# The passage from retention to the last MLP of a two-layer diffusion trunk: token chains in another order, two tokens scaled together, two weight units split earlier

## The chip, the cores and the metric

The kernel runs on one core of one Trainium2 chip, in float32. A core has a matrix engine (TensorE, PE in the profile, its weight loads PEld), three engines for element-wise work (VectorE or DVE, ScalarE or ACT, GpSimd or POOL) and SyncE (SP), which here only issues DMAs. Each engine works through its own queue in order. The metric is the device time of one execution in microseconds (us).

## The reference

Two layers work on 512 latent tokens of width 1024 and on 256 context tokens. Layer 0 mixes with neighbourhood attention and spatial gating, layer 1 with a bidirectional retention of 8 heads. After each mixer stands the same kind of MLP. What lies around the change, in full precision:

```
x = x + g1 * rmsnorm(y_lat, norm_g[i, 1])            # y_lat: output of the mixer
h = modulate(rmsnorm(x, norm_g[i, 2]), sh2, sc2)     # x * (1 + scale) + shift
x = x + g2 * rmsnorm(conv_ffn(h, ...), norm_g[i, 3])

def conv_ffn(h, w_in, conv_w, conv_b, w_out):        # w_in: 1024 x 5632, w_out: 2816 x 1024
    a = dwconv3(h @ w_in, conv_w, conv_b)            # three taps along the tokens
    gate, up = jnp.split(a, 2, axis=-1)
    return (silu(gate) * up) @ w_out
```

The retention ends in `(silu(g) * normed o) @ w_out`, with `w_out` of 2048 x 1024. The normalisations go over a token's whole width, so `h` of a token can be made only when its whole row of `y_lat` is there.

## The kernel before

**Precision and units.** Every float32 operand is split into a high and a low part, and every product is three matmuls, hi x hi, hi x lo and lo x hi (`mm3`, L152). `split` (L110) makes the two: ACT writes the high part, DVE the low one. A weight unit is 128 x 1024 numbers: loaded on SP into one of three `raw` buffers (`raw_unit`, L114), then split into a slot. In retention the slots are `w0` to `w5`, handed out in turn (`slot`, L133). `rv`, `sd`, `kd`, `gt` are retention's own tiles (values, scores, keys, gated output).

**The order on the engines.** The kernel is written in program order, and a planner with a model of the engines orders each queue: of what it takes to be ready it takes the earliest in the program. An instruction issued while its engine's `hold` flag is on is pinned behind the instruction traced before it on that engine:

```
def issue(*args, **kw):
    i = f(*args, **kw)
    if self.hold:
        self.tc.keep_in_program_order(i)
    return i
```

That is class `Ordered` (L61); `self.V`, `self.S` and `self.T` are DVE, ACT and PE through it, and `hold(on)` (L367) sets all three flags. GpSimd and SP have none.

**The passage.** `retention` (L1115) ends in `out_last` (L635). It has two feature groups, A (head 6) and B (head 7, whose weights `rwo7` it gets by a call), and four tiles of 128 tokens. For tokens 0 and 1 it makes A first and holds it in PSUM (`wrA`), then adds B; for tokens 2 and 3 it makes A and B together (`wrC`). After each half row it calls `final(t, y, n)` of the `finisher` (L650), under hold. Its steps for a token: `square_half` (ACT, sum of squares of a half), `gated_rows` (DVE, product with the gate, then GpSimd's reciprocal root `yd0r` to `yd3r`), `second` = `residual` (DVE adds to `xd`, ACT sums squares, the row is stored by a DMA on ACT's queue, GpSimd makes `xd0r` to `xd3r`), `third` = `normed` (half on DVE, half on ACT). `third` also puts building of the MLP's input on a list: pieces of `MLP_PIECES` (L37), as (half, tokens, first column, last of its half). A piece (`build_piece`, L483) is a generator: PE transposes (`ht`), scalings with shift into `sa` or `sb`, at the end of a half the splits into `hb` or `b`, and two adds. `fill(n)` (L409) runs n steps of the list, `need` (L404) all of a half; `FILLS` (L42) says how many steps follow each half row. With `split=True`, `out_last` flushes token 1 (its `second` and `third`) right after its last half row. `flush` at the end takes `between`, which loads and splits `wp101` and `wp011`; `early` does that for `wp001` before group B.

**The MLP.** `ffn` (L1439) replaces the product `h @ w_in` by seven products of half-size blocks, with block sums of the input (`block_sums`, L540, tiles `blk` and `hs`) and of the weights (units `wa`, `wb`, `wc`, in the first MLP `wd`). `plain` (L1595) does the first two column blocks without that: four groups `pf` on the first half of the features (units `wp001`, `wp101`, `wp011` and the unit of `f111r`), then four groups `pf..b` on the second half (tiles `b` and `hb`), and calls `block_sums` on the way. Then comes a loop over 20 blocks: X, Y, X, Z, X, Y, X of 12 matmuls each (`px`, `py`, `pz`), with pieces of the output product (`wf`) between them, and jobs of adaLN (`ag`, `ac`, `at`) now and then. The last groups go through `out_last` again (`wf0A` and so on).

Of the kernel before, what the change touches and what calls it, by code (L numbers as in the profile page):

```python
# [9 lines left out]
F32R = mybir.dt.float32r  # L10
# [3 lines left out]
ALU = mybir.AluOpType  # L14
AX = mybir.AxisListType

P = 128
# [7 lines left out]
NF = 22  # L25
# [8 lines left out]
EARLY = 2  # L34
# [1 line left out]
Q1, Q3 = 16, 48  # L36
MLP_PIECES = (  # L37
    ((0, (4, 5), 0, False), (0, (0,), 256, True), (1, (1,), 0, False), (1, (2,), 128, False), (1, (3,), 256, True)),
    ((0, (0,), 0, False), (0, (1,), 128, True), (1, (2,), 0, False), (1, (3,), 128, True)),
)  # L40

FILLS = {  # L42
    None: ((1, 1),) * 6,
    0: ((0, 0), (0, 0), (0, 0), (3, 2), (3, 2), (0, 3)),
    1: ((0, 0), (0, 0), (0, 3), (0, 5)),
}


# [30 lines left out]
class Trunk:  # L79
# [403 lines left out]
    def build_piece(self, l, half, toks, c0, last, xn, ab):  # L483
        S, V = self.S, self.V
        w = P * len(toks)
        s = 1 if toks[0] > 3 else 0
        q = 512 // w
        pts = {}

        def turn(kk):  # L490
            pt = pts[kk] = self.ps(f"ht{l}{toks[0]}{kk}", "BC"[kk % 2], (P, q, w))
            for i in range(q):
                k = q * kk + i
                for j, t in enumerate(toks):
                    self.T.transpose(pt[:, i, j * P : (j + 1) * P], xn[t][:, k * P : (k + 1) * P], self.ident)

        def scaled(kk):
            for i in range(q):
                k = q * kk + i
                A, B = ab[:, s, 0, k : k + 1], ab[:, s, 1, k : k + 1]  # L500
                h = self.staged(l, half, k, 1)[:, 0, c0 : c0 + w]
                if kk % 2 == 0:
                    S.activation(h, pts[kk][:, i, :], AF.Identity, scale=A, bias=B)
                else:
                    V.tensor_scalar(out=h, in0=pts[kk][:, i, :], scalar1=A, scalar2=B, op0=ALU.mult, op1=ALU.add)

        for kk in range(KD // q):
            if kk:
                scaled(kk - 1)
            turn(kk)  # L510
            yield
        scaled(KD // q - 1)
        yield
        if not last:
            return
        if half:
            n = self.bn
            self.b12 = [
                [self.xp.tile([P, 2, n], F32R, name=f"b12{l}{x}{m}", tag=f"g{x}", bufs=4 if l else 3) for m in range(2)]
                for x in range(2)  # L520
            ]
        for m in range(4):
            src = self.staged(l, half, 2 * m, 2)
            if half and m < 2:
                self.split(self.b12[0][m], self.b12[1][m], src)
            else:
                b = self.blk[(11, 21)[m // 2] if not half else 22]
                ks = slice(2 * (m % 2), 2 * (m % 2) + 2)
                self.split(b[:, 0, ks, :], b[:, 1, ks, :], src)
            if m % 2:  # L530
                yield
        if not half:
            for m in (0, 2):
                b11, b21 = (self.staged(l, 0, k + m, 2) for k in (0, 4))
                if l:
                    V.tensor_tensor(out=b21, in0=b21, in1=b11, op=ALU.add)
                else:
                    self.G.dma_start(b21, b11, accum_op=ALU.add)

    def block_sums(self, l):  # L540

        V, n = self.V, self.bn
        put = lambda b, m, src: self.split(b[:, 0, 2 * m : 2 * m + 2, :], b[:, 1, 2 * m : 2 * m + 2, :], src)
        st = [[self.staged(l, h, k + 2 * m, 2) for h in (0, 1) for k in (0, 4)] for m in range(2)]

        def add(out, x):
            if l:
                V.tensor_tensor(out=out, in0=out, in1=x, op=ALU.add)
            else:
                self.G.dma_start(out, x, accum_op=ALU.add)  # L550

        for m, (b11, b21, b12, b22) in enumerate(st):
            if l:
                t1 = self.t2k(f"t1{l}{m}", shape=(P, 2, n))
            else:
                t1 = self.bp.tile([P, 2, n], F32, name=f"t1{l}{m}", tag=f"y{1 + m}", bufs=1)
            V.tensor_tensor(out=t1, in0=b11, in1=b12, op=ALU.add)
            V.tensor_tensor(out=b22, in0=b22, in1=b12, op=ALU.add)
            put(self.blk["t", 1], m, t1)
            put(self.blk["t", 3], m, b22)  # L560
            if l:
                V.tensor_tensor(out=b12, in0=b22, in1=b21, op=ALU.add)
            else:
                add(b21, b22)
                self.G.dma_start(b12, b21)
            add(b22, b11)
            if l:
                yield
        if not l:
            yield  # L570
        hb = self.bp.tile([P, 6144 + Q1], F32R, name=f"hs{l}", tag="h1", bufs=1)
        for i, x in enumerate((2, 4)):
            self.blk["t", x] = hb[:, 8 * n * i : 8 * n * (i + 1)].rearrange("p (x k c) -> p x k c", x=2, k=4)
        self.rest = hb[:, 16 * n + Q1 : 16 * n + Q1 + 2048] if l else None
        for k, x in ((4, 2), (0, 4)):
            for m in range(2):
                put(self.blk["t", x], m, self.staged(l, 1, k + 2 * m, 2))
        yield
# [53 lines left out]
        for p in self.out_pieces(*args, **kw):  # L632
            p()

    def out_last(self, A, B, y, toks, early, final, name, split=False, between=None):  # L635

        e, o = toks[:early], toks[early:]
        held = {}
        self.out_group(*A, y, e, False, None, f"{name}A", "CB", held=held)
        if callable(B):  # L640
            B = B()
        if self.early:
            self.early()
        self.out_group(*B, y, e, False, final, f"{name}B", held=held)
        if split:
            final.flush()
        self.out_group(A[0] + B[0], A[1] + B[1], y, o, False, final, f"{name}C", "A")
        final.flush(between)

    def finisher(self, gates, src, ab, name, xts, last=False, mlp=None):  # L650
# [38 lines left out]
        def fin(t, y, n):  # L689
            if n == 0:  # L690
                begin(t, y)
                self.square_half(rows[-1], 0)
                if mlp is not None:
                    self.fill(steps[len(rows) - 1][0])
                if len(rows) > 1 and not state["flushed"]:
                    second(rows[-2])
                if mlp is None:
                    self.fill(steps[len(rows) - 1][0])
            else:
                self.square_half(rows[-1], 1)  # L700
                self.gated_rows(rows[-1])
                self.fill(steps[len(rows) - 1][1])
                if len(rows) > 1 and not state["flushed"]:
                    third(rows[-2])
                state["flushed"] = False

        state = {"flushed": False}

        def flush(between=None):

            self.hold(True)
            if between:
                between()
            second(rows[-1])
            if mlp is None:
                self.fill(2)
            third(rows[-1])
            self.hold(False)
            state["flushed"] = True

        fin.flush = flush
        return fin
# [392 lines left out]
    def retention(self, y, final):  # L1115
        S, V, T, G, a = self.S, self.V, self.T, self.G, self.a
        KS = float(np.float32(P) ** np.float32(-0.5))
        with ExitStack() as ctx:
# [226 lines left out]
            def w_out(h):  # L1345
                return [self.unit(a["ret_out"][(2 * h + f) * P : (2 * h + f + 1) * P], f"rwo{h}{f}") for f in range(2)]
# [3 lines left out]
            for h in range(8):  # L1350
# [69 lines left out]
                if h < 7:  # L1420
                    wk = qk(h + 1, 8, "k")
                else:
                    self.turn += 3
                    o6 = f, w_out(6)
                    self.bg_all()
                within(h, 0)
                across(h, 0)
                across(h, 1)
# [3 lines left out]
                across(h, 2)  # L1432
                across(h, 3)
                norm(h)
            self.out_last(o6, lambda: (gated(7), w_out(7)), y, toks, EARLY, final, "r", True, self.between)
            self.between = None


    def ffn(self, l, y, final, gates=None):  # L1439
# [13 lines left out]
        with ExitStack() as ctx:  # L1453
# [141 lines left out]
            def plain(js, steps):  # L1595
# [27 lines left out]
                for x, (j, i) in enumerate(order):  # L1623
# [4 lines left out]
                    ps[j, i] = [self.ps(f"pf{l}{i}{j}", "A", (P, n))]  # L1628
                    product(ps[j, i][0], d[j, i][0], hb(11), "open")
                    product(ps[j, i][0], d[j, i][1], hb(21), "close")  # L1630
                    self.hold(x < 2)
                    if x < 2:
                        self.fill(2)
                    self.hold(False)
                sums = self.block_sums(l)
                for j in js:
                    for i in range(2):
# [165 lines left out]
    def build(self):  # L1803
# [15 lines left out]

        def hook(*units):  # L1820
            def go():
                self.early = None
                for u in units:
                    ahead(*u)

            return go
# [28 lines left out]
        y = {}  # L1855
        xts = lambda: (self.xp, ("kd0", "kd1"), 1)

        self.early = hook(("wp001", ("ffn_in", 44), 2))
        self.between = hook(("wp101", ("ffn_in", 44 + NF), 0), ("wp011", ("ffn_in", 45), 1))
        self.retention(y, self.finisher(g3, xd, self.ab[1, 1], "d", xts, mlp=1))  # L1860
        g4 = self.gate_tiles(1, 2, 1)
        self.jobs = [self.ada_half(1, h, 1, g4, side=True) for h in (10, 11)]
# [112 lines left out]
```

## Time and profile before

| | us |
|---|---|
| median of 3 runs | 1856.04 (1852.79 to 1858.48) |
| the profiled execution | 1852.3 |
| its span, first to last instruction | 1850.5 |
| PE busy / PEld busy | 1781.8 / 1582.7 |
| DVE / ACT / POOL busy | 1391.1 / 1029.3 / 330.0 |
| first MLP's loop | from 435 to 897 |
| last `wrC` of retention starts to first product of the last MLP's loop | 1468.7 to 1510.2 |
| last MLP's loop | from 1510 to about 1819 |

In a timeline row stand the start and the length in us, the engine, the kernel's line (L71 is the helper `issue`, through which all PE, DVE and ACT instructions go), the operation, output<-inputs, the shape, the count of instructions merged, and in brackets the idle time of the engine before it with what ended it. In a row of windows stand the window and its length, then busy time with the number of instructions for PE, PEld, DVE, ACT and POOL, the granted PE clock as a share of full speed, the busy share of the DMA engines and GB/s. In a row of DMA issues stand output<-input, the queue, the count, the size and the median time from issue to landing.

### The profile page before, as it was taken

The page shows a single profiled execution, that of the slowest core. Times are in us where ns is not written, and L with a number is a line of the kernel's source. Part 1 is how long each engine was busy: PE and PEld are TensorE (multiplying, and loading weights), DVE is VectorE, ACT ScalarE, POOL GpSimd, SP SyncE. Part 2 cuts the span into 40 slices and gives each one's busy share as a digit, 9 for nine tenths or more (in the row PEclk, how much of TensorE's full clock was granted, in tenths as well). Part 3 has the DMA queues.
Part 4 walks back from the last instruction along what each step waited for, and adds up shares of the span by engine and source line. Part 5 has one row for each costly group of instructions (what it writes and reads, how often), then busy time and mean ns, then how long its engine had stood idle before and what let it go on. Part 6 is the DMA issues. An engine that isn't in the chain of part 4 may idle for free. (4 is left out here: it accounts for less than half of the span.)

```text
span 1850.5 us, 28777 instructions
## 1 busy us (share of the span) xinstructions
PE 1781.8 (96%) x10928; PEld 1582.7 (86%) x10928; DVE 1391.1 (75%) x2347; ACT 1029.3 (56%) x1866; POOL 330.0 (18%) x462
## 2 busy tenths in 40 slices
PE   7999899999999999999999999999999889999997
PEld 4888777679998899998888988988999789989996
DVE  4877675789878788787866676676656699988886
ACT  6533455677555565564664534344434467766763
POOL 1102122131122322222112011011101100222221
PEclk9999999999999999999999999999999989999999
DMA  7344321155577777786722422331321225877762
GB/s 297 112 141 143 117 82 36 55 171 148 178 156 168 174 175 161 156 173 151 265 97 92 143 99 80 125 113 58 105 69 60 101 82 157 215 197 201 171 161 97
DMA packets 84399, 253.45 MB, mean 137 GB/s; under 512 B 11026, under 2 KB 11538, under 8 KB 84260
## 3 DMA queue, kind: packets, MB, share of 16 engines
q1 hardware_dynamic: 55044, 191.27, 30.9%
q0 software_dynamic: 26912, 51.95, 16.4%
q10 hardware_dynamic: 2304, 8.39, 1.1%
q8 instruction: 86, 1.41, 0.3%
q14 instruction: 53, 0.43, 0.1%
HBM read 191.80 MB, written 39.85 MB: 125 GB/s over the span
## 5 line engine op out<-in xcount | busy, mean ns | idle before, releaser
L71 DVE SCALAR_TENSOR_TENSOR acc<-ar,cs,acc 128x512 f32<-128x512 f32 x256 | 185.7, 751 | 33.7 <-DMA ar<-in_adaw 24.7
L71 DVE SCALAR_TENSOR_TENSOR cv<-pre,cw,cv 128x769 f32<-128x769 f32 (+1 forms) x176 | 153.6, 884 | 4.9 <-ACT cv L71 4.2
L71 PE MATMUL rn<-rwv,h0c 128*128 128x256 f32 x768 | 136.3, 281 | 3.0 <-ACT h0c L71 3.0
L71 PEld LDWEIGHTS rn<-rwv,h0c 128*128 128x128 f32 x768 | 118.2, 191 | 3.7 <-ACT h0c L71 3.4
L71 PE MATMUL wf<-fo,g 128*128 128x512 f32 x432 | 112.6, 394 | 0.5 <-DVE fo L71 0.5
L71 PE MATMUL rn<-rwv,h1c 128*128 128x256 f32 x384 | 108.1, 282 | 0.4 <-DVE h1c L71 0.2
L1688 POOL DMA_DIRECT2D yf<-yp x64 | 55.1, 861 | 257.0 <-ACT yp L71 233.8
L71 ACT ACTIVATE cv<-pre,cw 128x770 f32<-128x770 f32 (+1 forms) x88 | 81.3, 925 | 24.0 <-DVE pre L71 23.4
L71 PE MATMUL rn<-rwg,h0c 128*128 128x256 f32 x512 | 90.0, 280 | 0.0
L71 PEld LDWEIGHTS wf<-fo,g 128*128 128x128 f32 x432 | 75.9, 188 | 13.8 <-DVE fo L71 1.4
L71 PE MATMUL px<-hs,wc 128*128 128x384 f32 (+1 forms) x480 | 79.3, 314 | 5.4 <-ACT pre L71 3.2
L71 PEld LDWEIGHTS px<-hs,wc 128*128 128x128 f32 x480 | 74.3, 191 | 10.8 <-ACT pre L71 5.4
L71 ACT ACTIVATE pre<-px 128x256 f32<-128x256 f32 (+2 forms) x160 | 54.3, 367 | 47.7 <-PE px L71 47.6
L71 ACT COPY yp<-wf 128x512 f32<-128x512 f32 x118 | 67.8, 576 | 19.0 <-PE wf L71 16.5
L71 PEld LDWEIGHTS rn<-rwg,h0c 128*128 128x128 f32 x512 | 78.1, 189 | 0.0
L71 PE MATMUL pz<-hb,wa 128*128 128x384 f32 (+1 forms) x480 | 77.3, 308 | 0.0
L71 PE MATMUL px<-hb,wa 128*128 128x384 f32 (+1 forms) x480 | 77.1, 308 | 0.0
L71 PE MATMUL py<-blk,wb 128*128 128x384 f32 (+1 forms) x480 | 76.9, 308 | 0.0
L71 PE MATMUL px<-blk,wb 128*128 128x384 f32 (+1 forms) x480 | 76.7, 309 | 0.0
L71 PEld LDWEIGHTS px<-hb,wa 128*128 128x128 f32 x480 | 73.2, 188 | 3.2
L71 PEld LDWEIGHTS px<-blk,wb 128*128 128x128 f32 x480 | 73.4, 189 | 3.0 <-ACT pre L71 0.2
L71 PEld LDWEIGHTS rn<-rwv,h1c 128*128 128x128 f32 x384 | 72.9, 190 | 1.5 <-DVE h1c L71 1.3
(1272 smaller groups left out, 5112.6 us busy)
## 6 DMA issues: line engine op xcount, KB each, us to landing
ar<-in_adaw SPq DMA_DIRECT2D x96, 512.0 KB, 3.9
yf<-yp POOLq DMA_DIRECT2D x64, 256.0 KB, 4.2
yd<-yp POOLq DMA_DIRECT2D x54, 256.0 KB, 5.0
yd<-ypg POOLq DMA_DIRECT2D x54, 256.0 KB, 4.9
fin<-xd SPq DMA_DIRECT2D x8, 512.0 KB
xn<-in_x SPq DMA_DIRECT2D x6, 512.0 KB, 4.6
xb<-in_x SPq DMA_DIRECT2D x6, 512.0 KB
xd<-xb ACTq DMA_DIRECT2D x6, 512.0 KB, 2.8
```

The source lines that it names most:

```text
L71: i = f(*args, **kw)
L1688: G.dma_start((yd[t] if first else y[t])[:, o], v, accum_op=ALU.add)
```

## The change

- Token chains: the flush of token 1 amid `out_last` goes (`split`, `flushed`). Each token's `second` and `third` now run while the next token's half rows come in, and in this passage the filling follows `third`. The five steps that complete the first half follow token 3's first half row and no longer its second.
- The pieces of tokens 2 and 3 become one of 256 columns.
- `wp101` and `wp011` are loaded and split in head 7, ahead of its `within` (`self.ahead()`), no longer in the last flush. For that `rwo7` leaves the slots `w0` and `w1`: its first unit goes into head 7's `rv` tiles, its second, in two halves, into the `sd` tiles.
- In layer 1 the adds `b21 += b11` (two) and `b22 += b11` (two) go from DVE to accumulating DMAs on GpSimd's queue, as layer 0 has them.
- In `plain`, filling between the `pf` groups remains for the first MLP alone; the lines that set `hold` move with it.

```
-    ((0, (0,), 0, False), (0, (1,), 128, True), (1, (2,), 0, False), (1, (3,), 128, True)),
+    ((0, (0,), 0, False), (0, (1,), 128, True), (1, (2, 3), 0, True)),
 ...
-    1: ((0, 0), (0, 0), (0, 3), (0, 5)),
+    1: ((0, 0), (0, 0), (0, 3), (5, 0)),
 ...
             for m in (0, 2):
                 b11, b21 = (self.staged(l, 0, k + m, 2) for k in (0, 4))
-                if l:
-                    V.tensor_tensor(out=b21, in0=b21, in1=b11, op=ALU.add)
-                else:
-                    self.G.dma_start(b21, b11, accum_op=ALU.add)
+                self.G.dma_start(b21, b11, accum_op=ALU.add)
 ...
-            add(b22, b11)
+            self.G.dma_start(b22, b11, accum_op=ALU.add)
 ...
         if self.early:
             self.early()
+            self.early = None
         self.out_group(*B, y, e, False, final, f"{name}B", held=held)
-        if split:
-            final.flush()
         self.out_group(A[0] + B[0], A[1] + B[1], y, o, False, final, f"{name}C", "A")
         final.flush(between)
 ...
-                if len(rows) > 1 and not state["flushed"]:
+                if len(rows) > 1:
                     second(rows[-2])
 ...
                 self.gated_rows(rows[-1])
-                self.fill(steps[len(rows) - 1][1])
-                if len(rows) > 1 and not state["flushed"]:
+                if mlp != 1:
+                    self.fill(steps[len(rows) - 1][1])
+                if len(rows) > 1:
                     third(rows[-2])
-                state["flushed"] = False
+                if mlp == 1:
+                    self.fill(steps[len(rows) - 1][1])
 ...
                     o6 = f, w_out(6)
                     self.bg_all()
+                    self.ahead()
                 within(h, 0)
 ...
-            self.out_last(o6, lambda: (gated(7), w_out(7)), y, toks, EARLY, final, "r", True, self.between)
+            def last_out():
+                u = [rp.tile([P, 1536], F32R, name=f"wo7{x}", tag=f"rv{x}", bufs=1)[:, :1024] for x in range(2)]
+                halves = [[rp.tile([P, 512], F32R, name=f"wo7s{x}{n}", tag=f"sd{x}", bufs=2) for n in range(2)] for x in range(2)]
+                rows = [self.raw_unit(a["ret_out"][(14 + f) * P : (15 + f) * P], f"rwo7{f}") for f in range(2)]
+                self.split(u[0], u[1], rows[0])
+                for n in range(2):
+                    self.split(halves[0][n], halves[1][n], rows[1][:, 512 * n : 512 * n + 512])
+                return [u, [Halves(x) for x in halves]]
+
+            self.out_last(o6, lambda: (gated(7), last_out()), y, toks, EARLY, final, "r", self.between)
 ...
                     product(ps[j, i][0], d[j, i][0], hb(11), "open")
                     product(ps[j, i][0], d[j, i][1], hb(21), "close")
-                    self.hold(x < 2)
-                    if x < 2:
+                    if first and x < 2:
+                        self.hold(True)
                         self.fill(2)
-                    self.hold(False)
+                        self.hold(False)
 ...
-        self.between = hook(("wp101", ("ffn_in", 44 + NF), 0), ("wp011", ("ffn_in", 45), 1))
+        self.ahead = hook(("wp101", ("ffn_in", 44 + NF), 0), ("wp011", ("ffn_in", 45), 1))
```

More of the change, by code (lines that the diff above doesn't have):

```diff
@@ L544, in block_sums @@
         st = [[self.staged(l, h, k + 2 * m, 2) for h in (0, 1) for k in (0, 4)] for m in range(2)]
[L546 to L550, printed above, removed]
         for m, (b11, b21, b12, b22) in enumerate(st):
@@ L563, in block_sums @@
             else:
-                add(b21, b22)
+                self.G.dma_start(b21, b22, accum_op=ALU.add)
                 self.G.dma_start(b12, b21)
-            add(b22, b11)
+            self.G.dma_start(b22, b11, accum_op=ALU.add)
             if l:
@@ L633, in out_group, with out_last @@
             p()
-    def out_last(self, A, B, y, toks, early, final, name, split=False, between=None):
+    def out_last(self, A, B, y, toks, early, final, name, between=None):
         e, o = toks[:early], toks[early:]
@@ L701, in fin @@
                 self.gated_rows(rows[-1])
-                self.fill(steps[len(rows) - 1][1])
-                if len(rows) > 1 and not state["flushed"]:
+                if mlp != 1:
+                    self.fill(steps[len(rows) - 1][1])
+                if len(rows) > 1:
                     third(rows[-2])
-                state["flushed"] = False
-        state = {"flushed": False}
+                if mlp == 1:
+                    self.fill(steps[len(rows) - 1][1])
         def flush(between=None):
@@ L718, in flush @@
             self.hold(False)
-            state["flushed"] = True
         fin.flush = flush
@@ L1821, in go @@
             def go():
-                self.early = None
                 for u in units:
```

## The prediction

> **What bounds the kernel now.** I read the page first, then the table of windows by stage, then the timeline of the passage engine by engine. The page's lines of engine totals and of DMA issues that I use, with one of a list of DMA issues around 400 us:
>
> ```profile
> span 1850.5 us, 28777 instructions
> PE 1781.8 (96%) x10928; PEld 1582.7 (86%) x10928; DVE 1391.1 (75%) x2347; ACT 1029.3 (56%) x1866; POOL 330.0 (18%) x462
> yf<-yp POOLq DMA_DIRECT2D x64, 256.0 KB, 4.2
> sa<-sa POOLq DMA_DIRECT2D x2, 384.0 KB, 7.0
> ```
>
> The windows (length, then busy us of each engine with its count, granted clock, DMA share, GB/s):
>
> ```profile
> 600.00:800.00 200.00, 198.23 (x1027) 182.41 (x1026) 162.11 (x234) 115.89 (x198) 52.05 (x66) 0.99 0.77 168
> 640.63:644.04 3.41, 3.41 (x11) 2.92 (x10) 3.41 (x7) 2.64 (x4) 1.21 (x2) 0.50 0.88 208
> 1475.00:1482.00 7.00, 1.00 (x5) 0.47 (x3) 6.52 (x15) 5.49 (x16) 1.96 (x5) 0.88 0.26 106
> 1480.31:1487.14 6.83, 5.83 (x25) 5.54 (x26) 6.83 (x12) 4.87 (x8) 0.43 (x1) 0.50 0.07 8
> 1517.86:1524.68 6.82, 5.84 (x24) 5.36 (x25) 6.82 (x11) 3.45 (x6) 0.00 (x0) 0.50 0.26 77
> 1560.00:1835.00 275.00, 272.62 (x1877) 251.11 (x1876) 237.52 (x370) 184.56 (x329) 59.10 (x71) 1.00 0.71 179
> ```
>
> TensorE (PE) bounds nearly everything: 99% in the first MLP's loop (600 to 800) and in the last one's (1560 to 1835), so a microsecond that PE loses there is a microsecond of the end. The passage is the exception: one busy us of seven from 1475, then 6.8 us at clock 0.50, and once more from 1517.86. PE's rows there, with the idle time before each:
>
> ```profile
> 1468.73 5.71 PE L71 MATMUL wrC<-rwo,gt 128*128 128x512 f32 x24
> 1474.27 1.04 PE L71 MATMUL ht<-ident,yr 128*128 128x128 f32 x8
> 1481.16 6.00 PE L71 MATMUL pf<-hb,wp 128*128 128x256 f32 x24 [5.85 <-ACT hb L71]
> 1496.12 2.90 PE L71 MATMUL pf<-hb,wp 128*128 128x256 f32 x22 [0.74 <-DVE wp L71]
> 1498.85 0.28 PE L71 MATMUL pf100b<-b,wp 128*128 128x256 f32 x1
> ...
> 1513.33 1.41 PE L71 MATMUL pz<-hb,wa 128*128 128x256 f32 x11
> 1517.84 0.58 PE L71 MATMUL px<-hs,wc 128*128 128x256 f32 x1 [2.18 <-ACT wc L71]
> 1520.10 1.65 PE L71 MATMUL px<-hs,wc 128*128 128x256 f32 x6
> ```
>
> There are two holes: 5.85 us before the first `pf` (the tokens' scaled and split halves are late), and the wait for `hs` and `wc` at 1517.84, after which the same product really runs from 1520.10.
>
> **The change part by part.**
>
> *Token chains.* Rows of VectorE (DVE), ScalarE (ACT) and its queue (ACTq):
>
> ```profile
> 1471.12 0.49 DVE L71 TENSOR_SCALAR yr<-xd,xd1r 128x512 f32<-128x512 f32 x1 [1.89 <-POOL xd1r L329]
> 1471.52 1.28 DVE L71 TENSOR_TENSOR yr<-wrC,yr 128x512 f32<-128x512 f32 x2
> 1473.06 1.31 DVE L71 TENSOR_TENSOR yr<-yr,G 128x512 f32<-128x512 f32 x2 [0.25 <-ACT jyd L71]
> ...
> 1488.28 0.33 ACTq L71 DMA_DIRECT2D xd<-xd  x1
> 1493.75 1.06 ACT L71 ACTIVATE wp<-f111r 128x1024 fp32r<-128x1024 f32 x1 [2.95 <-DMA xd<-xd]
> 1494.84 1.23 DVE L71 TENSOR_TENSOR wp<-f111r,wp 128x1024 fp32r<-128x1024 f32 x1 [3.64 <-ACT wp L71]
> ...
> 1514.36 0.69 DVE L71 TENSOR_TENSOR sb<-sb,sa 128x512 f32<-128x512 f32 x1
> 1519.35 0.69 DVE L71 TENSOR_TENSOR hs<-sb,hs 128x512 fp32r<-128x512 f32 x1
> ```
>
> Today token 1 is finished in one go, so token 2's two adds and two gate products (1.28 + 1.31) stand behind a 1.89 us wait for GpSimd's `xd1r`, with their results long in PSUM. Laced, they run inside that wait, and what follows comes about 2.6 us sooner. The five steps of tokens 0/1 now precede token 2's residual: `pf` starts near 1477, not 1481.16, which leaves a hole of 1 to 2 us before it, as the last `wrC` ends a little later than now (the eight `ht` of row 1474.27 move in between). Out of DVE's way there go also the two moved splits (1.2 each, the form of row 1494.84) and an add into `sa` (0.69, the form of row 1514.36). Token 3's residual lands about 3.5 us sooner. Bounds: 0.7 (one add alone) and 5.7 (2.6 + 2.4 + 0.7); I take 3.5, from walking the pinned DVE order with these durations, since token 2's residual now stands behind the splits. Its store, issued at 1488.28, keeps `wp<-f111r` waiting until 1493.75, 5.5 us. This stays, as do the pinned scales behind it.
>
> *Last two tokens together.* Eight scalings of 256 columns take the place of sixteen of 128; saved DVE and ACT time, about 1 us each, lies behind the same wait. PE must now do all 16 transposes between the third and fourth `pf` group, when it waits anyway. No change on the path.
>
> *Two weight units and `ret_out` 7.* `wp101` and `wp011` go to the place where `rwo70` and `rwo71` are split today, early in head 7, in exchange for the same work: cost nothing. But `rwo7` must wait for head 7's `rv` and `sd` tiles, that is for its last `ro` product, and as its raw tiles hold two of three buffers, `wp001` (split at 1428.61 today) follows it. Three units' low halves, 3 x 1.23 = 3.7 us of DVE, come into the stretch of these rows:
>
> ```profile
> 1428.61 1.23 DVE L71 TENSOR_TENSOR wp<-wp001r,wp 128x1024 fp32r<-128x1024 f32 x1 [2.53 <-ACT wp L71]
> 1454.00 0.73 DVE L71 TENSOR_SCALAR on<-of,rmv,rrr 128x256 f32<-128x256 f32 x2 [0.86 <-POOL rrr L1309]
> 1456.55 1.41 DVE L71 SCALAR_TENSOR_TENSOR gt<-rt,gng,gt 128x512 fp32r<-128x512 f32 x2 [1.14 <-ACT gt L71]
> 1458.59 0.69 DVE L71 TENSOR_TENSOR yr<-wrA,yr 128x512 f32<-128x512 f32 x1 [0.63 <-PE wrA L71]
> ```
>
> The gaps shown hold 2.6 us of the 3.7, so token 0's add is late by 1.1 at most, by 0.4 if the chain's own order shields it; I take 0.8. The first `b` product then starts 2.7 us sooner.
>
> *Adds on GpSimd's DMA queue.* Four DVE adds of 0.69 leave. The last, at 1514.36, is also the last reader of the memory that `hs` takes. A DMA of this size lands in 4.2 us (`yf<-yp`), up to 7.0 (`sa<-sa`, larger). DVE has 4.3 us of other work between the rows at 1514.36 and 1519.35, so 4.2 is covered and 7.0 would cost 2.7. With two of the adds gone from the queue after `b` the product of 1520.10 starts near 1516.8 (2.7 + 1.4 - 0.8 for `hs` work bunched behind the DMA).
>
> *The order of PE.* This is no part of the change's name. In `plain` the closing `self.hold(False)` moves inside `if first and x < 2`; after the last of the four products `T.hold` stays on, and nothing clears it until the first `out_pieces` of `out_last`. So all PE instructions of both MLP loops are pinned to program order. In the steady loops the trace has that order already: nothing. At three places it hasn't. PE and ACT in the first MLP:
>
> ```profile
> 437.17 2.28 PE L71 MATMUL py<-blk,wb 128*128 128x384 f32 x12
> 439.29 2.28 PE L71 MATMUL pz<-hb,wa 128*128 128x384 f32 x12
> 441.96 0.73 PE L71 MATMUL wf<-fo00h,g 128*128 128x512 f32 x2 [0.39 <-ACT fo00h L71]
> 443.12 2.38 PE L71 MATMUL px<-hs,wc 128*128 128x384 f32 x12 [0.43 <-ACT pre L71]
> ...
> 639.72 0.50 PE L71 MATMUL wf<-fo09l,g 128*128 128x512 f32 x1 [1.77 <-DVE fo09l L71]
> ...
> 884.62 0.87 PE L71 MATMUL pz<-hb,wa 128*128 128x384 f32 x4
> 886.50 2.38 PE L71 MATMUL px<-hs,wc 128*128 128x384 f32 x12 [1.01 <-ACT pre L71]
> ...
> 897.40 0.40 PE L71 MATMUL wf0A<-fo018h,g 128*128 128x512 f32 x1
> 898.18 0.56 ACT L71 COPY arow<-ac 2x512 f32<-2x512 f32 x1
> 898.89 0.41 PE L71 MATMUL at<-ident,arow 2*128 2x2 f32 x4
> ```
>
> In program order `px<-hs` stands ahead of `pz`. It can't start before 443.12 (ACT `pre`, one buffer), so PE stands idle from 439.29, 3.8 us, and the 12 `pz` (2.1 us, as the 12 `py` from 437.17 to 439.29) and two `wf` (some 0.4) come after: +2.5. At 884.62 four `pz` (0.7) do the same: +0.7. `at` must follow `ac` at once and wait for the copy that starts at 898.18; the six `wf0A` between 897.40 and 898.89 (1.4) come after: +1.4. Together +4.6; below that 0, if ACT and DVE come in another order, and never a gain, as PE has no other work to take. In the last MLP what PE does from 1513.33 to the start of the hole (1517.84 - 2.18 = 1515.66), 2.3 us, comes after the wait; about 1 us more of the product's work falls to half clock, 0.5. Against them stand the 3.3 us by which that product is sooner: -0.5 for the whole passage. Bounds: -15 with both holes (5.85 + 2.18) and their half clock (2 x 3.4) gone, +4 with the DMA late.
>
> The hole of 3.8 us also costs clock. After the 1.77 us wait at 639.72 the clock stood at 0.50 for 3.41 us (row 640.63): 1.7 us lost; after the passage's holes for 6.8, 3.4 lost each time. I take 1.7.
>
> The Trainium skill, "TensorE: Matmul & The Clock Gate", section "What's actually happening", says that the array falls to half rate after an idle window of about 3.4 us of a free-running counter. Here a hole of half that was enough, so the trace decides against needing a whole window; by the page's rule a 3.8 us hole would rarely cover one and the sum would be 1.7 us lower.
>
> Sum: 4.6 + 1.7 - 0.5 = +5.8 us. The profiled execution took 1852.3 us and would take 1858.1; it stands 3.7 under the median of 1856.04, which becomes 1862.
>
> **The rivals.** *Faster:* the passage's second hole closes. If the DVE queue from 1494.84 runs 6 us sooner rather than 3.3, `px<-hs` is ready when `py` ends and PE meets neither hole nor half clock. For it: 4 adds and 2 splits, 5.2 us, leave DVE. Against: the store's 5.5 us stands before that queue. Gain 15, less 6.3 for the pin: 1848. It decides once `px<-hs` starts before 1513.
>
> *No change:* the pin costs 2.5 to 4.6 without half clock and the passage gives 2 to 4: 1855 to 1859. For it: the clock's loss hangs on where the hole falls.
>
> *Slower still:* the POOL-queue adds land after 7 us and `hs` is late by 2.7, with another 1.5 at half clock: near 1866. Against: `yf<-yp` lands in 4.2 beside a busy DVE. The Trainium skill, "SBUF — State Buffer", section "SBUF: two separate sides", has a rule for it: DVE in a two-port mode keeps GpSimd from writing descriptors. DVE is busy 6.82 of 6.82 us in the window from 1517.86, so the page would favour this rival.
>
> **How the numbers follow.** Chances: forecast 0.40 (of it 0.35 over the bound, 0.05 within), no change 0.30, faster 0.15, slower still 0.15. A measurement of this kernel tells about 0.3% (5.6 us) from no change. Slower 0.35 + 0.15 = 0.50, same 0.35, faster 0.15. The range runs from 1851, which leaves out most of the faster rival, to 1868, which takes in 1866 and a second 6.8 us clock stretch; the forecast's own is 1859 to 1865.
>
> **What would show it.** Right: in the first MLP's second step `px<-hs` directly after `py`, after a hole near 4 us, with a clock of 0.5 behind it; `at` directly after `ac`; the hole before `pf` under 2 us; the first `b` product some 3 us sooner from the end of retention; `px<-hs` ahead of `pz` in the last MLP. Wrong: PE order as before in the first MLP, or first `b` product sooner by 6, or the last MLP's loop with new waits.

## The result, and the profile after

The changed kernel takes 1864.92 us (median of 10 runs), the kernel before, in as many runs beside it, 1853.03. The ratio is 1.0068, with an interval of 1.0054 to 1.0083: slower by 10 to 15 us, where the prediction had 5.8. The page of the changed kernel (span; busy time by engine):

```profile
span 1863.5 us, 28784 instructions
PE 1787.7 (96%) x10928; PEld 1588.4 (85%) x10928; DVE 1390.4 (75%) x2340; ACT 1030.9 (55%) x1863; POOL 333.2 (18%) x466
```

PE does as many matmuls as before, and its busy time grows by 5.9 us: part of the loss is products at half clock. The changed kernel's windows (columns as before) show where:

```profile
436.68:440.09 3.41, 1.22 (x7) 0.89 (x6) 3.41 (x5) 3.41 (x7) 0.00 (x0) 1.00 0.00 0
440.09:446.92 6.83, 5.54 (x17) 5.54 (x18) 6.50 (x8) 3.79 (x8) 0.00 (x0) 0.50 0.32 82
1475.00:1482.00 7.00, 7.00 (x40) 5.78 (x39) 6.57 (x15) 5.37 (x14) 2.62 (x5) 1.00 0.43 157
1491.41:1494.82 3.41, 1.94 (x18) 1.71 (x16) 1.41 (x2) 1.45 (x4) 0.97 (x3) 1.00 0.36 103
1515.30:1518.71 3.41, 0.85 (x5) 0.65 (x5) 3.41 (x6) 1.24 (x4) 0.88 (x1) 1.00 0.19 35
1518.71:1528.95 10.24, 6.12 (x26) 5.76 (x27) 9.49 (x15) 6.17 (x11) 0.00 (x0) 0.50 0.35 110
1535.77:1539.18 3.41, 3.41 (x15) 3.12 (x15) 3.41 (x5) 2.76 (x6) 0.00 (x0) 0.50 0.05 18
1560.00:1835.00 275.00, 270.49 (x1894) 250.51 (x1893) 234.52 (x365) 186.17 (x328) 57.34 (x68) 1.00 0.72 178
```

From 1475 to 1482, where PE was busy 1.00 us of 7.00 before, it is now busy throughout, and the half clock at 1480 is gone. Three losses are new where PE's order changed: a half clock of 6.83 us in the first MLP's second step, 10.24 us of it where there had been 6.83 at the start of the last MLP's loop, and 3.41 more behind that. Other windows of half clock come and go elsewhere: 3.41 us each at 576.63, 863.35, 1003.29 and 1016.95 here and at 640.63 before. The pin isn't their cause, as `unpin` below, without it, has two of them too (574.47 and 861.19). PE's timeline at these places:

```profile
435.79 2.10 PE L71 MATMUL py<-blk,wb 128*128 128x384 f32 x11
441.38 4.21 PE L71 MATMUL px<-hs,wc 128*128 128x384 f32 x12 [3.49 <-ACT pre L71]
445.39 2.78 PE L71 MATMUL pz<-hb,wa 128*128 128x384 f32 x11
...
1484.18 0.38 PE L71 MATMUL pf<-hb,wp 128*128 128x256 f32 x1 [0.74 <-ACT hb L71]
1495.72 1.86 PE L71 MATMUL ht<-ident,yr 128*128 128x128 f32 x15 [2.37 <-DVE yr L71]
1498.52 2.90 PE L71 MATMUL pf<-hb,wp 128*128 128x256 f32 x22 [0.70 <-DVE wp L71]
1501.25 1.58 PE L71 MATMUL pf100b<-b,wp 128*128 128x256 f32 x12
...
1515.32 0.85 PE L71 MATMUL py<-blk,wb 128*128 128x256 f32 x5 [0.31 <-DVE blk L71]
1521.78 0.79 PE L71 MATMUL px<-hs,wc 128*128 128x256 f32 x2 [5.60 <-ACT wc L71]
1523.62 2.64 PE L71 MATMUL px<-hs,wc 128*128 128x256 f32 x10 [1.05 <-DVE wc L71]
1526.06 2.76 PE L71 MATMUL pz<-hb,wa 128*128 128x256 f32 x12
1535.38 2.62 PE L71 MATMUL px<-hs 128*128 128x256 f32 x12 [2.31 <-DVE pre L71]
```

Both MLPs show the pinned order: `px<-hs` behind `py`, and `pz` only after it. In the last MLP PE waits 5.60, 1.05 and 2.31 us, 9.0 together, where before it waited 2.18 and 0.98.

To split the difference I take two stretches of each profile, by the starts of PE rows: *first MLP*, from the first `py` of its loop (437.17 before) to the start of `py`'s 33rd product with `wc` (494.50 before); *passage*, from head 7's last `rx` (1448.77 before) to the last matmul, with two marks on its way. Before, they take 57.3 and 392.0 us. The changed kernel's are 62.0 and 398.3. The 10.9 us of both are most of the 13.0 by which the spans differ; the rest is spread over the stretches between, in pieces of at most 3 us, the largest at the windows just named.

| kernel | ratio (95% interval) | first MLP | first `b` product | first `px<-hs` of the last MLP | passage |
|---|---|---|---|---|---|
| before | 1 | 57.3 | 50.1 | 69.1 | 392.0 |
| changed | 1.0068 (1.0054–1.0083) | 62.0 | 46.1 | 66.6 | 398.3 |
| unpin0 | 1.0037 (1.0020–1.0054) | 57.3 | 47.4 | 67.9 | 399.0 |
| unpin1 | 1.0007 (0.9991–1.0023) | 61.0 | 46.1 | 66.6 | 390.9 |
| unpin | 0.9982 (0.9965–0.9999) | 57.3 | 46.7 | 67.2 | 389.9 |
| dve | 1.0066 (1.0040–1.0093) | 61.2 | 50.7 | 68.7 | 400.8 |
| pin | 1.0076 (1.0058–1.0094) | 62.3 | 49.8 | 68.9 | 401.3 |
| oldlace | 0.9989 (0.9976–1.0002) | 57.5 | 49.2 | 67.2 | 390.4 |
| oldunits | 0.9994 (0.9980–1.0007) | 57.8 | 49.9 | 70.5 | 394.4 |
| mix | 0.9975 (0.9962–0.9987) | 57.9 | 46.0 | 66.5 | 389.9 |
| zfirst | 1.0054 (1.0036–1.0072) | 59.4 | 47.4 | 69.0 | 400.3 |
| oldpieces | 0.9997 (0.9981–1.0013) | 57.1 | 48.9 | 69.8 | 391.8 |
| unpin_dve | 1.0000 (0.9986–1.0014) | 57.5 | 50.7 | 68.7 | 390.6 |
| mixpool | 0.9975 (0.9963–0.9986) | 57.5 | 46.1 | 64.9 | 387.6 |

Each ratio is against the kernel before in executions beside it. The columns behind the ratio are us of one profiled execution; the marks count from the start of the passage. In `unpin0`, `zfirst` and `oldpieces` a half clock of 3.41 us starts at 1461 to 1468, ahead of all in which their passage differs from the changed kernel's or `unpin`'s, and lengthens the passage and its marks by 1.3 to 1.6 us.

### The profile page after: what moved, and what is told of

It is laid out like the page before. It is cut to its first block, busy times and chain, and to the rows that moved or that the text cites. A ratio compares the mean times of both kernels' runs of the same rounds, so it can differ in the third digit from the quotient of the medians.

```text
span 1863.5 us, 28784 instructions
## 1 busy us (share of the span) xinstructions
PE 1787.7 (96%) x10928; PEld 1588.4 (85%) x10928; DVE 1390.4 (75%) x2340; ACT 1030.9 (55%) x1863; POOL 333.2 (18%) x466
```

## The experiments

Theory: the flag that stays on, and so the pinned order of PE, is the loss. Rivals: GpSimd's DMA adds make `hs` late; the new order of chains and units itself costs; or the loss in the first MLP is the clock's chance.

### The flag cleared: first MLP, last MLP, both

Behind the loop over the four `pf` groups in `plain` (for unpin0 `if first`, for unpin1 `if not first`):

```diff
+                self.hold(False)
                 sums = self.block_sums(l)
```

> The changed kernel, but the TensorE flag is cleared after plain's loop in the first MLP; the last MLP stays pinned. The median of the kernel before is taken as 1853.0 us, the changed kernel stands 12.6 us above it (ratio 1.0068). Theory pin: the offset between the two traces goes from -1.56 to +3.08 us at the first MLP's second step (a hole of 3.65 us ahead of px<-hs, then 6.83 us at half clock) and by another 1.4 us near 878, so this kernel is 4.6 to 6 us faster than the changed one: 7 to 8 us above before, ratio about 1.004. Rival chance: that offset is a matter of where the clock's window falls, and this kernel stands where the changed one does, 1.0068 within 0.15%. PE in the first MLP should show pz and two wf ahead of px<-hs and no half clock near 440.

> The changed kernel, but the TensorE flag is cleared after plain's loop in the last MLP; the first MLP stays pinned. Theory pin: in the last MLP the offset goes from +2.4 us at the first product to +11.7 at the second block; some 31 matmuls (3.6 us), a second hole of 2.3 us ahead of px<-hs at 1535.38 and 3.4 us of extra half clock go with the pin, so this kernel is 6 to 9 us faster than the changed one, 4 to 7 us above before: ratio 1.002 to 1.0035. Rival adds: hs comes late because of the GpSimd DMA (issued 1516.77, landed 1520.05), which stays here; then only the 2.3 us of pz that fit into the hole come back and the ratio stays at 1.0055.

> The changed kernel with the TensorE flag cleared after plain's loop in both MLPs, so nothing of the pin is left. Theory pin: both parts together, 11 to 15 us faster than the changed kernel, ratio 0.9985 to 1.001 against before. Rival adds: 7 us faster, ratio 1.003. Rival chains (the new order itself is what costs, the pin only moves work): above 1.004.

Clearing it in the first MLP takes 0.31% (5.8 us) off the changed kernel, in the last MLP 0.61% (11.3), in both 0.86% (15.9), each to some 0.2%, as two intervals go into it. The traces show 4.7 us in the first MLP (`unpin0`), 7.3 in the passage (`unpin1`), and 4.7 and 8.4 in `unpin`. The rivals of chance (no gain in the first MLP) and of the adds (2.3 us in the last) fall. The kernel with both cleared is no slower than before but some 0.2% faster, by an interval that barely leaves out 1: the new order isn't what costs. Its PE rows in the last MLP:

```profile
1510.88 0.99 PE L71 MATMUL py<-blk,wb 128*128 128x256 f32 x7
1511.70 0.40 PE L71 MATMUL pz<-hb,wa 128*128 128x256 f32 x2
1512.17 0.85 PE L71 MATMUL py<-blk,wb 128*128 128x256 f32 x5
1512.86 1.30 PE L71 MATMUL pz<-hb,wa 128*128 128x256 f32 x10
1514.00 0.63 PE L71 MATMUL wf<-fo,g 128*128 128x512 f32 x2
...
1518.63 0.50 PE L71 MATMUL px<-hs,wc 128*128 128x256 f32 x2 [3.54 <-ACT wc L71]
1519.67 0.56 PE L71 MATMUL py<-hb,wc 128*128 128x256 f32 x2 [0.54 <-ACT wc L71]
1520.48 1.43 PE L71 MATMUL px<-hs,wc 128*128 128x256 f32 x5 [0.25 <-DVE wc L71]
...
1531.66 1.52 PE L71 MATMUL px<-hs 128*128 128x256 f32 x12
```

PE is held up for 4.3 us (3.54, 0.54, 0.25) against 9.0, as it puts `pz`, `wf` and the next `px` before the wait, `py<-hb,wc` between the parts of a product whose operands come piecemeal, and other work ahead of the second `px<-hs`. That is 4.6 us. At half clock PE was busy for 6.12 + 3.41 us in the changed kernel, and for 3.16 us behind this wait in `unpin` (3.41 us long); half of the difference, 3.2 us, is lost. Together they make up most of the 8.4 us between the two passages (398.3 and 389.9).

### The flag alone

```diff
-                    self.hold(False)
+                    self.V.hold = self.S.hold = False
+                    T.hold = x >= 2
```

That is the kernel before, in `plain`.

> The kernel before, with nothing changed but that the TensorE flag stays on after plain in both MLPs, as in the changed kernel. Theory pin (clearing the flag took the changed kernel from 1.0068 to 0.9982): 12 to 17 us slower than before, ratio 1.0065 to 1.009, with px<-hs directly behind py in the first MLP's second step after a hole near 4 us, and directly behind py in the last MLP. Rival, pin only together with the GpSimd adds: in the last MLP hs comes some 3 us sooner here than in the changed kernel, so the pin costs less, ratio 1.004 to 1.005.

It is 0.76% slower than before, about as slow as the whole change (1.0068): the first MLP's stretch is 5.0 us longer, the passage 9.3. The pin needs none of the rest of the change to cost this, and the rival by which it costs less without GpSimd's adds falls. PE rows:

```profile
434.78 2.28 PE L71 MATMUL py<-blk,wb 128*128 128x384 f32 x12
440.91 4.21 PE L71 MATMUL px<-hs,wc 128*128 128x384 f32 x12 [3.85 <-ACT pre L71]
...
1520.69 1.81 PE L71 MATMUL py<-blk,wb 128*128 128x256 f32 x12
1526.84 0.58 PE L71 MATMUL px<-hs,wc 128*128 128x256 f32 x1 [4.34 <-ACT wc L71]
1529.09 1.65 PE L71 MATMUL px<-hs,wc 128*128 128x256 f32 x6 [1.67 <-DVE hs L71]
1541.62 2.61 PE L71 MATMUL px<-hs 128*128 128x256 f32 x12 [2.32 <-DVE pre L71]
```

### The pin kept, the hole filled by the program's own order

```diff
+                if j == 2:
+                    product(Z, d[12], hb(21), "only")
                 product(X, d["q", 3], hb(("t", 2)), "onto")
-                product(Z, d[12], hb(21), "only")
+                if j > 2:
+                    product(Z, d[12], hb(21), "only")
```

> The changed kernel with the flag left on, as it is, but in the first block after plain in both MLPs the 12 pz stand in the program ahead of the 12 px<-hs, so that the pinned order itself fills the hole. Theory pin (the cost is what PE can't do while it waits for px<-hs): 2.1 us come back in the first MLP, 1.4 in the last, and up to 3.4 of half clock; 3.5 to 7 us faster than the changed kernel, ratio 1.003 to 1.005; the second hole of the last MLP, ahead of px<-hs at 1535.38, stays. Rival, the pin costs by the order later in the loops (wf, the second block): under 1.5 us faster, ratio above 1.006.

In the first MLP half of the loss comes back (59.4 us, between 57.3 and 62.0): the hole is 2.06 us and no half clock follows. In the last MLP nothing does: it still waits 4.25, 1.05 and 2.86 us, with 10.24 us at half clock. PE rows of `zfirst`:

```profile
444.31 2.35 PE L71 MATMUL px<-hs,wc 128*128 128x384 f32 x12 [2.06 <-ACT pre L71]
...
1527.40 0.80 PE L71 MATMUL px<-hs,wc 128*128 128x256 f32 x2 [4.25 <-ACT wc L71]
1541.34 1.65 PE L71 MATMUL px<-hs 128*128 128x256 f32 x12 [2.86 <-DVE pre L71]
```

The ratio of 1.0054 stands between the two expectations, and its interval holds the changed kernel's value. One fixed order was no remedy here, where several products wait in turn.

### The adds

In `dve` (flag on) and `unpin_dve` (flag cleared) the four adds of layer 1 go back to DVE; in `mix` (flag cleared) only the two of `block_sums`:

```diff
-            self.G.dma_start(b22, b11, accum_op=ALU.add)
+            if l:
+                V.tensor_tensor(out=b22, in0=b22, in1=b11, op=ALU.add)
+            else:
+                self.G.dma_start(b22, b11, accum_op=ALU.add)
```

> The changed kernel, pins included, with the four adds of layer 1 back on DVE. Theory pin: hs comes some 3 us sooner, but the products stay pinned behind it; 2 to 3 us faster than the changed kernel, ratio 1.0055. Rival adds: the whole late start of px<-hs and its half clock go, 6 to 9 us faster, ratio 1.002 to 1.0035. If DVE is the tighter queue the adds cost what the DMA costs: ratio 1.0068, no change.

> Flag cleared in both MLPs, and all four adds of layer 1 back on DVE. With the flag on, the adds on DVE made the way from retention's last rx to the end 400.8 us against 398.3. Theory early adds (two more adds stand ahead of the wp split and the b split in the DVE queue, and PE waits there): 2 to 3 us slower than the kernel with only the flag cleared, ratio 0.9985 to 1.000, first b product 3 to 4 us later. Rival, TensorE free to choose hides it: 0.9975 to 0.9985.

> Flag cleared in both MLPs; the two adds inside block_sums (b22 += b11) on DVE, the two early ones (b21 += b11) on GpSimd's queue as in the changed kernel. Theory late add: the wait for hs (3.7 us ahead of px<-hs, DMA issued after blk and landed 3.3 us later) shortens by 1.5 to 3 us while nothing is added to DVE ahead of the b split; 1.5 to 4 us faster than the kernel with only the flag cleared, ratio 0.996 to 0.9975. Rival, wc and hs on ACT and DVE are late by their own queues: no change, 0.998 to 0.999.

With the flag on the ratio shows no difference, 1.0066 against 1.0068, neither the 2 to 3 us of gain that the theory had nor the 6 to 9 of the rival; the passage of the trace is 2.5 us longer. The rival on which GpSimd's DMAs are the loss falls. The marks show a trade. With all adds on DVE the first `b` product comes 4.0 to 4.6 us later, since PE waits longer for the `ht` of the last tokens and then for `wp`, with half clock from 1494.69 for 6.83 us. Rows of `unpin_dve`, to be held against the waits of 2.37 and 0.70 us above:

```profile
1493.57 2.45 PE L71 MATMUL ht<-ident,yr 128*128 128x128 f32 x15 [3.68 <-DVE yr L71]
1498.24 4.32 PE L71 MATMUL pf<-hb,wp 128*128 128x256 f32 x22 [1.79 <-DVE wp L71]
...
1520.42 0.38 PE L71 MATMUL px<-hs,wc 128*128 128x256 f32 x1 [1.33 <-ACT wc L71]
```

In exchange `hs` no longer waits for a DMA, and PE stands before it for 1.33 us and not 3.54; the first `px<-hs` comes 1.5 us later than with the DMAs. Mixing the two was to give both gains. `mix` is at 0.9975, inside the interval of `unpin`, and its `px<-hs` comes 0.7 us sooner, as much as the first `b` product does, so nothing is gained behind that. The ratio lies at the edge of what the theory had, but the trace speaks for the rival, by which `wc` and `hs` are late by the queues of DVE and ACT.

### The other parts, with the flag cleared

`oldlace` puts back the flush of token 1 and the filling behind token 3's second half row; `oldunits` the two units in the last flush and `rwo7` in its slots; `oldpieces` two pieces for tokens 2 and 3. The lines that say it:

```diff
-    1: ((0, 0), (0, 0), (0, 3), (5, 0)),
+    1: ((0, 0), (0, 0), (0, 3), (0, 5)),
...
+        if split:
+            final.flush()
```

```diff
-        self.ahead = hook(("wp101", ("ffn_in", 44 + NF), 0), ("wp011", ("ffn_in", 45), 1))
+        self.ahead = lambda: None
+        self.between = hook(("wp101", ("ffn_in", 44 + NF), 0), ("wp011", ("ffn_in", 45), 1))
...
-            self.out_last(o6, lambda: (gated(7), last_out()), y, toks, EARLY, final, "r", self.between)
+            self.out_last(o6, lambda: (gated(7), w_out(7)), y, toks, EARLY, final, "r", self.between)
```

```diff
-    ((0, (0,), 0, False), (0, (1,), 128, True), (1, (2, 3), 0, True)),
+    ((0, (0,), 0, False), (0, (1,), 128, True), (1, (2,), 0, False), (1, (3,), 128, True)),
```

> Flag cleared in both MLPs, and token 1 flushed in one go again with the five filling steps behind token 3's second half row; the merged pieces, the moved units and the GpSimd adds stay. Theory laced chains give the gain (hole ahead of pf 0.9 us with them, 6.0 before, and no half clock there): the hole of some 6 us is back, 5 to 9 us slower than the kernel with only the flag cleared (0.9982), ratio 1.001 to 1.003. Rival, the moved splits close the hole by themselves (3.7 us of DVE and ACT work gone from the chain): the hole stays under 3 us and the ratio under 0.9995.

> Flag cleared in both MLPs, and the two weight units back in the last flush with ret_out 7 in its old slots; laced chains, merged pieces and GpSimd adds stay. Theory of the prediction: two splits of 1.2 us on DVE come back ahead of the last token's chain, and 2.5 us of stalls ahead of the A and B products (rt, wrA) go; first b product 0 to 3 us later, 0 to 3 us slower than the kernel with the flag cleared, ratio 0.998 to 1.000. Rival, the moved rwo7 costs more in the stretch before it than it saves behind it: ratio 0.996 to 0.998.

> Flag cleared in both MLPs, and the last two tokens as two pieces of 128 columns again; the rest of the change stays. Theory of the prediction, no change on the path: within 1 us of the kernel with only the flag cleared, ratio 0.9975 to 0.999, the passage from retention's last rx to the end 389 to 391 us. Rival, merging two tokens is what makes PE wait 2.5 us ahead of ht (both tokens have to be there) and its going is a gain: 2 us faster, ratio below 0.9975; or eight more scalings on DVE and ACT come ahead of the b split: 1 to 2 us slower, 0.999 to 1.000.

All three ratios lie above that of `unpin`, but every interval meets its own, so the runs don't settle what each part is worth; the traces tell what it does. PE rows of `oldlace`, then of `oldunits`:

```profile
1484.97 1.03 PE L71 MATMUL ht<-ident,yr 128*128 128x128 f32 x8
1491.32 11.29 PE L71 MATMUL pf<-hb,wp 128*128 128x256 f32 x72 [5.32 <-ACT hb L71]
```

```profile
1479.53 0.38 PE L71 MATMUL pf<-hb,wp 128*128 128x256 f32 x1 [0.74 <-ACT hb L71]
1487.60 0.79 PE L71 MATMUL pf<-hb,wp 128*128 128x256 f32 x2 [4.45 <-ACT wp L71]
```

The laced chains alone close the hole before `pf`: 5.32 us without them, 0.74 with them, wherever the units are. Still the passage is only 0.5 us shorter for it (390.4 and 389.9), because the first `px<-hs` starts at 67.2 in both, and PE's lead of 2.5 us at the `b` product is spent waiting there. What it waits for comes through DVE (busy 10.00 of 10.00 us from 1515 in `oldlace`), the last DMA add and ACT; `mixpool` below, with less on DVE, starts it sooner. So the hole came back as expected, and the 5 to 9 us expected with it did not. The moved units are needed as well: with the laced chains and the units in the flush, PE runs into `wp`, 4.45 us. They are worth most in the trace, 4.5 us of passage, though they have a price ahead of it: the first `wrC` starts 15.2 us after the last `rx` and 13.7 in `oldunits`. In `oldpieces` the half clock ahead of what differs is 1.6 of its 1.9 us: by the trace the merged pieces change next to nothing. The ratio of 0.9997 lies where the second rival had it (eight more scalings, 1 to 2 us), which the runs don't rule out.

### A version with less on DVE

`mixpool` is `mix` with the two sums `t` of `block_sums` on GpSimd:

```diff
-            V.tensor_tensor(out=t1, in0=b11, in1=b12, op=ALU.add)
+            (self.G if l else V).tensor_tensor(out=t1, in0=b11, in1=b12, op=ALU.add)
```

> As the mixed kernel (flag cleared, late adds on DVE, early ones on GpSimd's queue), and the two sums t = sa + sb of block_sums as instructions of GpSimd and not of DVE. Theory DVE bounds this stretch (busy 10.0 of 10.0 us from 1510): 1.4 us of DVE go and hs comes sooner by 1 to 1.5, ratio 0.9965 to 0.9975. Rival, GpSimd's instruction takes longer than the 0.69 us of DVE and slows DVE beside it, and py waits for blk: 1 to 3 us slower than the mixed kernel, ratio 0.998 to 0.9995.

`px<-hs` starts 1.6 us sooner than in `mix`, and the passage is the shortest of all, 387.6. It isn't free: GpSimd's two sums take 1.35 us each, and the split of `b` that DVE begins beside them takes 1.84 us, in `mix` 1.28. Rows of GpSimd and DVE:

```profile
1499.22 2.69 POOL L548 TENSOR_TENSOR t<-sa,sb 128x512 f32<-128x512 f32 x2 [3.04 <-ACT sb L71]
1501.22 1.84 DVE L71 TENSOR_TENSOR b<-sb,b 128x512 fp32r<-128x512 f32 x2
```

The ratio is 0.9975 for both, so the runs can't tell them apart; both beat the kernel before and the changed one.

## Why the prediction was right or wrong

The direction, and its main cause, were right: the prediction found that `T.hold` stays on, though the change's name says nothing of it, and named it as the loss. The size was off by a factor of two, from one term, with a smaller error the other way. The time itself, 1864.92 us, comes nearer to the forecast 1862 than the step does only because the kernel before took 1853.03 us beside it and not 1856.04: that part is luck.

- *Pin, first MLP.* At its second step: predicted 2.5 for order and 1.7 for clock, 4.2; the stretch grows by 4.6 in the changed kernel (62.0 against 57.3, before rounding 4.63), and by 3.6 to 5.0 in the three others pinned there in the same order. The hole is 3.49 us as forecast (3.8). The half clock is 6.83 us and not 3.41; in `pin` it is 6.83 too, in `unpin1` and `dve` 3.41 as forecast, so which of the two comes is chance.
- *The other two places there* (0.7 and 1.4): not seen. From the loop's first `py` to the eighth `wf0C<-fo,g` the changed kernel takes 484.9 us and the one before 479.8, 5.1 against the 4.6 above. At 888 three `wf0A` stand ahead of `px<-hs` in program order and fill most of its wait (1.39 us left). `at` was not right behind `ac`, though the prediction had named that as a sign of being right: six `wf0A` stood between, so nothing waited.
- *Pin, last MLP.* This is the step that failed, and with it one of the prediction's own signs of being wrong came about, new waits in the last MLP's loop. The prediction put 2.3 us of work behind the wait and 0.5 of clock, 2.8 in all. It measured 8.4 (changed against `unpin`) and 9.3 (`pin` against before). The step counted only what PE did before the hole of 1517.84. It left out that in the trace of before PE went on with other products between the parts of `px<-hs`, the `py<-hb,wc` from 1519.40, and that the next block's `px<-hs`, which waited for nothing before, then waits for `pre`, 2.31 us more. PE rows of before:

```profile
1519.40 0.80 PE L71 MATMUL py<-hb,wc 128*128 128x256 f32 x2 [0.98 <-ACT wc L71]
1521.55 1.27 PE L71 MATMUL py<-hb,wc 128*128 128x256 f32 x5
1532.52 1.52 PE L71 MATMUL px<-hs 128*128 128x256 f32 x12
```

- *Laced chains.* `pf` was put near 1477 with a hole of 1 to 2 us; counted from the last `rx` it starts at 29.0 and not 32.4, which is 1477.8 on the clock of before, with 0.74 and 0.34 us of waiting. The first `b` product was to come 2.7 us sooner and comes 4.0 sooner.
- *`px<-hs` 3.3 us sooner:* its start is 2.5 sooner, its main part (1523.62, before 1520.10) 2.9. That is less than the `b` products gained, because `hs` waits for the last DMA add. Rows of DVE, GpSimd and ACT in the changed kernel's timeline:

```profile
1515.79 0.69 DVE L71 TENSOR_TENSOR blk<-sb,blk 128x512 fp32r<-128x512 f32 x1
1516.77 0.88 POOL L557 DMA_DIRECT2D sb<-sa  x1 [7.84 <-DVE blk L71]
1520.05 1.15 ACT L71 ACTIVATE hs<-sb 128x512 fp32r<-128x512 f32 x2 [0.87 <-DMA sb<-sa]
```

- *The adds' landing.* The DMA issued at 1516.77 has landed when ACT goes on at 1520.05, 3.3 us later, below the 4.2 assumed: the rival "slower still" with 7 us fell, though the time lies near its 1866 (luck again). DVE was busy 3.41 of 3.41 us from 1515.30 (windows above), and the DMA was no later for it. The Trainium skill, "SBUF — State Buffer", section "SBUF: two separate sides", speaks of DVE in a two-port mode. The prediction took DVE's busy time for that; no run here shows the mode, so the rule is neither borne out nor refuted.
- *The rival "faster":* it needed `px<-hs` before 1513; on the clock of before it starts at 1515.4. Its 1848 adds up to 1847.
- *Units and merged pieces at nothing on the path:* right for the pieces as far as the trace tells. For the units it missed that they are what keeps PE from the wait of 4.45 us once the chains are laced, so the parts belong together.

The sum with the measured terms: 4.6 for the first MLP, 8.4 for the last MLP's pin, less 2.2 gained by the rest of the passage (392.0 to 389.9), +10.8. The ratio's 0.68% is 12.6 us, and 10.8 lies inside its interval. It is no separate proof, as by the way these terms are taken they add up to the 10.9 of the two stretches above.

## What to carry to other kernels

Look for the state that a changed line used to reset: here a closing call that moved under a condition pins an engine for two whole loops, and it costs more than the named parts of the change give. Where a planner fills waits with other work, pricing a fixed order takes all the work that ran between the parts of the waiting products, over every wait until the steady loop, and the half clock behind each hole. Ahead of a stretch that another engine bounds, a closed hole is worth only what that engine's queue lets through.

## What was not expected of the hardware

The half clock follows a rule that can be read from the rows. Every stretch, but for the one that the end of the span cuts off, lasts 3.41 us or a multiple of it, and what decides is how long PE stood idle in the 3.41 us just before, not the length of the hole. The same wait for `ht`, 2.37 us in the changed kernel and 2.36 in `unpin`, fell across two of these windows in the one (1491.41 to 1494.82 above: 1.94 of 3.41 busy, and full clock after it) and into one window in the other. Windows of `unpin`:

```profile
1489.25:1492.66 3.41, 1.05 (x10) 0.83 (x10) 0.75 (x2) 2.08 (x6) 0.86 (x2) 1.00 0.37 154
1492.66:1496.07 3.41, 3.41 (x19) 3.41 (x18) 2.59 (x5) 3.41 (x8) 0.00 (x0) 0.50 0.65 189
```

I laid each profile's grid of 3.41 us over PE's rows, in the fourteen profiles from 200 us on, without the end of the span. Of windows at full clock, all 76 with more than 1.9 us of idle time were followed by half clock, 15 of 80 with 1.3 to 1.9, and none of some 6,470 with less. The Trainium skill, "TensorE: Matmul & The Clock Gate", section "What's actually happening", states the free-running window of 3413 ns, which agrees; an idle window as the condition is too strict here, as about half a window was enough. So a single hole under 1.3 us cost no clock here, and one of 2 to 3 us did or didn't by where it fell. The executions of one kernel fit that: among the 29 of the kernel before beside `unpin`, the mean granted clock lies between 0.986 and 0.992 and the time between 1851.9 and 1865.8 us, the longer times mostly at the lower clock (correlation -0.78). That the place of the windows is the reason wasn't tried.
